# Rotary embedding and attention scores: the first batch in 24 KB stores, an early load on ScalarE's ring, and an uneven last store

## The chip, the cores and the metric

One core of a Trainium2 chip runs the kernel. The metric is the device time of one execution in microseconds (us). Runs of a kernel scatter by some 0.2 per cent here, so each comparison rests on five or six runs of a kernel with the kernel before run beside it. Instants are counted from the start of the profiled span, as in the views.

## The reference

For 16 batches of 512 positions, 16 heads of 64 numbers, q and k are rotated by tables of cosines and sines, and for each position and head the products with all 512 rotated k of that head are written out: 67 MB are read, 268 MB are written, all in float32.

```python
batch, seq, heads, dim = 16, 512, 16, 64
q_rot = concat([q1*cos - q2*sin, q1*sin + q2*cos])      # k_rot likewise
scores = einsum('bshd,bthd->bsht', q_rot, k_rot)         # (16, 512, 16, 512)
```

## The kernel before

The 512 positions of a batch lie as 128 partitions x 4 "slots". VectorE (DVE) rotates, TensorE (PE) transposes and multiplies, ScalarE (ACT) copies the products from PSUM to a staging buffer, and SyncE (SP) stores it: 4 MB for each of 64 slots, 32 KB per partition. There are three staging buffers of 4 MB. In the first batch one of them first holds the early inputs. A semaphore counts what has landed of each transfer: a "landing" is the moment at which one of the 16 DMA engines has finished its part, and "the median engine" is the middle of the 16. A "ring" is the queue of transfers that one issuing engine (SP or ScalarE) feeds.

```python
stage_pool = ctx.enter_context(tc.tile_pool(name="stage", bufs=3))
st_first = [stage_pool.tile([P, H, S], fp32, tag="stage", name="st") for _ in range(2)]
early = stage_pool.tile([P, 2 * C * H * D], fp32, tag="stage", name="early")
# ... cut
for head, heads in ((0, G), (G, H - G)):      # 4 heads of all rows, then 12
    load_units("k", head, heads)              # all on nc.sync
    load_units("q", head, heads)
load("k", 1); load("q", 1)
# ... cut; in scores(), first batch: unit i is 4 heads of all four slots, 1 MB per slot
if b == 0 and p % 2 == 1:
    c = p // 2
    nc.sync.dma_start(o_v[0, c, :, G * i : G * (i + 1)], st[:, G * c : G * (c + 1)])
elif b > 0 and p == HP - 1:
    nc.sync.dma_start(o_v[b, i % C], st)      # 4 MB
```

## Time and profile before

| | |
|---|---|
| Time, median of the runs beside the changed kernel | 802.22 us |
| Span of the profiled run | 799.2 us |
| Busy: PE, ACT, DVE | 86, 70, 68 per cent |
| DMA | 336.17 MB, mean 421 GB/s |

The views that bound it stand in the prediction. Two more are needed as a base for comparison. The first is DVE's timeline near 10 us (start, duration, engine, line, operation; in brackets the idle time before it and who ended it):

```profile
8.05 1.29 DVE L111 TENSOR_TENSOR early<-early,part 128x512 f32<-128x512 f32 x2
9.38 1.23 DVE L106 TENSOR_TENSOR part<-early,ss_t 128x1024 f32<-128x1024 f32 x1
```

The second is a table of short windows; its last two columns are the mean busy share of the 16 DMA engines and GB/s. Between 28 and 36 us, and about 60 us, the DMA engines are full:

```profile
28.00:30.00 2.00, 2.00 (x14) 0.91 (x12) 1.55 (x3) 1.42 (x3) 0.00 (x0) 1.00 1.01 430
30.00:32.00 2.00, 2.00 (x13) 1.14 (x12) 2.00 (x3) 1.36 (x2) 0.00 (x0) 1.00 1.08 426
32.00:34.00 2.00, 2.00 (x12) 0.99 (x12) 1.93 (x4) 1.91 (x4) 0.00 (x0) 1.00 0.88 377
34.00:36.00 2.00, 2.00 (x13) 0.77 (x10) 1.93 (x4) 2.00 (x4) 0.00 (x0) 1.00 1.04 430
...
60.00:62.00 2.00, 2.00 (x16) 1.31 (x16) 1.93 (x3) 2.00 (x4) 0.00 (x0) 1.00 1.03 422
```

### The profile page before, as it was taken

The numbers are of one execution on the slowest core, as the hardware profiler recorded it, in microseconds if no ns is written. First come the engines' busy times: TensorE is split into PE (matmuls) and PEld (weight loads), VectorE is DVE, ScalarE is ACT, GpSimd is POOL, SyncE is SP. The second block draws the span as 40 slices with busy tenths as digits, with TensorE's granted clock in tenths as the row PEclk, the third lists the DMA queues.
The fourth block names the chain that finished last, engine by engine and source line by source line (L and its number), as shares of the span: only waits on it lengthen the run. The fifth ranks groups of instructions, "written<-read, shape, count | busy, mean of one in ns | idle before, by whom it ended". The sixth has DMA issues, their size and how long they took to land.

```text
span 799.2 us, 7712 instructions
## 1 busy us (share of the span) xinstructions
PE 690.9 (86%) x3072; PEld 299.7 (37%) x3072; DVE 544.6 (68%) x516; ACT 561.8 (70%) x647; POOL 0.7 (0%) x6
## 2 busy tenths in 40 slices
PE   4989998997979789797897978979789897889970
PEld 2444443443434334343343433434334343334420
DVE  7999987676858568585684866848668586685300
ACT  3878886776848578585775856768567685667870
POOL 0000000000000000000000000000000000000000
PEclk9999999899989899898998989989899898998995
DMA  9999999999999999999999999999999999998995
GB/s 353 420 426 430 431 416 430 426 433 440 424 438 423 428 435 424 442 425 433 427 433 431 432 431 429 433 433 424 426 428 435 433 402 430 438 426 362 429 422 249
DMA packets 17700, 336.17 MB, mean 421 GB/s; under 512 B 1792, under 2 KB 3072, under 8 KB 4096
## 3 DMA queue, kind: packets, MB, share of 16 engines
q1 hardware_dynamic: 17376, 335.55, 98.4%
q8 instruction: 24, 0.39, 0.2%
q10 hardware_dynamic: 288, 0.13, 0.1%
q14 instruction: 12, 0.10, 0.0%
HBM read 67.24 MB, written 268.44 MB: 420 GB/s over the span
## 4 chain that ended last, share of the span: by engine, by line
DMA 50%; PE 37%; DVE 5%; ACT 4%; issue 1%; ACTq 0%; DVEq 0%
DMA out_dram<-st 49%; PE ps L155 28%; PE bank L127 9%; ACT st L162 4%; DVE part L106 2%; DVE early L111 1%; DVE k_sb L107 1%; DVE k_sb L111 1%; DVE early L107 1%; DMA early<-in_k_dram 1%; DVE kT_t L142 0%; DVE q_sb L107 0%; DVE q_sb L111 0%; ACTq L270 0%; DVE qT_t L142 0%
## 5 line engine op out<-in xcount | busy, mean ns | idle before, releaser
L162 ACT COPY st<-ps 128x1024 f32<-128x1024 f32 x512 | 495.3, 1018 | 202.8 <-DMA out_dram<-st 113.9
L155 PE MATMUL ps<-kT_t,qT_t 64*128 64x512 f32 x2048 | 548.6, 654 | 70.9 <-ACT st L162 70.9
L155 PEld LDWEIGHTS ps<-kT_t,qT_t 64*128 64x128 f32 x2048 | 185.4, 198 | 258.9 <-issue 138.9
L142 DVE COPY qT_t<-bank 128x512 f32<-128x512 f32 x118 | 81.6, 691 | 202.4 <-PE bank L127 202.4
L127 PEld LDWEIGHTS bank<-ident,q_sb 128*128 128x128 f32 x480 | 55.6, 152 | 104.5 <-issue 101.9
L127 PE MATMUL bank<-ident,q_sb 128*128 128x128 f32 x480 | 86.8, 309 | 0.9 <-PE ps L155 0.9
L127 PEld LDWEIGHTS bank<-ident,k_sb 128*128 128x128 f32 x480 | 50.5, 141 | 95.1 <-DVE k_sb L107 38.0
L127 PE MATMUL bank<-ident,k_sb 128*128 128x128 f32 x480 | 78.7, 287 | 1.6 <-DVE qT_t L142 1.2
L142 ACT COPY kT_t<-bank 128x512 f32<-128x512 f32 x122 | 72.4, 597 | 6.2 <-PE bank L127 6.2
L107 DVE TENSOR_TENSOR q_sb<-q_sb,cos_t 128x1024 f32<-128x1024 f32 x60 | 73.5, 1225 | 2.1
L111 DVE TENSOR_TENSOR k_sb<-k_sb,part 128x1024 f32<-128x1024 f32 x60 | 73.5, 1225 | 2.1
L107 DVE TENSOR_TENSOR k_sb<-k_sb,cos_t 128x1024 f32<-128x1024 f32 x60 | 73.5, 1225 | 2.0
L106 DVE TENSOR_TENSOR part<-q_sb,ss_t 128x1024 f32<-128x1024 f32 x60 | 73.5, 1225 | 2.0
L106 DVE TENSOR_TENSOR part<-k_sb,ss_t 128x1024 f32<-128x1024 f32 x60 | 73.0, 1216 | 0.1
L111 DVE TENSOR_TENSOR q_sb<-q_sb,part 128x1024 f32<-128x1024 f32 x60 | 72.9, 1216 | 0.0
L127 PE MATMUL bank<-ident,early 128*128 128x128 f32 x64 | 10.5, 316 | 12.2 <-DVE early L111 10.3
L127 PEld LDWEIGHTS bank<-ident,early 128*128 128x128 f32 x64 | 8.3, 161 | 17.6 <-issue 14.3
L106 DVE TENSOR_TENSOR part<-early,ss_t 128x1024 f32<-128x1024 f32 x8 | 9.8, 1223 | 5.7 <-ACT ss_t L187 5.5
L111 DVE TENSOR_TENSOR early<-early,part 128x512 f32<-128x512 f32 x16 | 10.3, 687 | 0.2
L107 DVE TENSOR_TENSOR early<-early,cos_t 128x1024 f32<-128x1024 f32 x8 | 9.8, 1224 | 0.3
L142 ACT COPY qT_t<-bank 128x512 f32<-128x512 f32 x10 | 5.6, 615 | 3.2 <-PE bank L127 3.2
L142 DVE COPY kT_t<-bank 128x512 f32<-128x512 f32 x6 | 4.1, 685 | 1.3 <-PE bank L127 1.3
(9 smaller groups left out, 2.8 us busy)
## 6 DMA issues: line engine op xcount, KB each, us to landing
out_dram<-st SPq DMA_DIRECT2D x60, 4096.0 KB, 25.0
k_sb<-in_k_dram SPq DMA_DIRECT2D x15, 2048.0 KB, 28.4
q_sb<-in_q_dram SPq DMA_DIRECT2D x15, 2048.0 KB, 27.5
out_dram<-st SPq DMA_DIRECT2D x16, 1024.0 KB, 13.0
early<-in_k_dram SPq DMA_DIRECT2D x1, 1536.0 KB, 9.1
early<-in_q_dram SPq DMA_DIRECT2D x1, 1536.0 KB, 12.3
early<-in_k_dram SPq DMA_DIRECT2D x1, 512.0 KB, 4.7
early<-in_q_dram SPq DMA_DIRECT2D x1, 512.0 KB, 5.4
```

Of the source, the lines that this page charges most:

```text
L106: nc.vector.tensor_tensor(pv, xs, ss, op=mult)
L107: nc.vector.tensor_tensor(xc, xc, cs, op=mult)
L111: nc.vector.tensor_tensor(y, y, z, op=add)
L127: nc.tensor.transpose(bank[:, x, :], src, ident)
L142: copy(out=dst, in_=src)
L155: nc.tensor.matmul(out=po, lhsT=lhs[64 * r : 64 * r + 64, :], rhs=rh, start=True, stop=True)
L162: nc.scalar.copy(out=so, in_=si)
```

## The change

It has three parts with three aims (`...` marks what is left out): larger store packets in the first batch (four heads of all slots first, then the other twelve heads slot by slot, 24 KB per partition); an earlier start (the first 0.5 MB of q is issued by ScalarE, on its own ring, beside SP's); and a shorter end (part of the last store is given to few DMA engines, so that a slow one has less to do).

```diff
-            load_units("k", head, heads)
-            load_units("q", head, heads)
+            load_units(nc.sync, "k", head, heads)
+            load_units(nc.scalar if head == 0 else nc.sync, "q", head, heads)
...
+        dve = rope("k", 1) + rope("k", 2) + rope("k", 3) + rope("r", 0)
+        for p in range(HP):                    # four heads of all slots
+            c, hp = divmod(p, 2)
+            scores(qT["q", 0][:, C * hp + c], kT[0][:, hp], st_first[0][:, 2 * p : 2 * p + 2], True)
+            if hp == 1:
+                nc.sync.dma_start(o_v[0, c, :, :G], st_first[0][:, G * c : G * (c + 1)])
+            if p in (3, 7):
+                load("kq"[p // 4], 2)
...
         for i in range(C):                     # twelve heads, slot i
-            st = st_first[i] if i < 2 else stage_pool.tile(...)
+            st = st_first[1] if i == 0 else stage_pool.tile(...)
...
+            for p in range(2, HP):
+                scores(qT["r", i][:, p], kT[0][:, p], st[:, 2 * p : 2 * p + 2], True)
...
+            nc.sync.dma_start(o_v[0, i, :, G:], st[:, G:])
...
+    def store(i, st):
+        o = o_v[i // C, i % C]
+        if i < NST - 1:
+            nc.sync.dma_start(o, st)
+            return
+        h = H - 2
+        nc.sync.dma_start(o[:, :h], st[:, :h])
+        nc.sync.dma_start(o[:116, h:], st[:116, h:])
+        nc.sync.dma_start(o[116:, h:], st[116:, h:])
```

## The prediction

> **What bounds the kernel now.** I read the page's slices first, then the DMA issues, the end of the span in windows of 2 us, the landing events of each transfer, and the timelines of SP, ACT and PE in the first 80 us.
>
> ```profile
> DMA  9999999999999999999999999999999999998995
> GB/s 353 420 426 430 431 416 430 426 433 440 424 438 423 428 435 424 442 425 433 427 433 431 432 431 429 433 433 424 426 428 435 433 402 430 438 426 362 429 422 249
> ...
> HBM read 67.24 MB, written 268.44 MB: 420 GB/s over the span
> ```
>
> The DMA engines are full from the second slice to the last but one, at some 430 GB/s, with no compute engine over 86% busy. So it is a DMA kernel, and only three things can move its time: bytes or packets, stretches in which an engine has nothing queued, and the ends. The change alters no bytes. The end is the odd part:
>
> ```profile
> 787.00:789.00 2.00, 0.00 (x0) 0.00 (x0) 0.00 (x0) 0.00 (x0) 0.00 (x0) 0.50 0.87 377
> 789.00:791.00 2.00, 0.00 (x0) 0.00 (x0) 0.00 (x0) 0.00 (x0) 0.00 (x0) 0.50 0.69 295
> 791.00:793.00 2.00, 0.00 (x0) 0.00 (x0) 0.00 (x0) 0.00 (x0) 0.00 (x0) 0.50 0.08 33
> 793.00:795.00 2.00, 0.00 (x0) 0.00 (x0) 0.00 (x0) 0.00 (x0) 0.00 (x0) 0.50 0.08 33
> ```
>
> The last two columns are DMA share and GB/s: for some 7 us a share near 1/16 is left, that is one engine, sending 32 KB packets one after another (1213 ns each in the trace). I call it the straggler. Each transfer raises its semaphore once for each engine, so the 16 landings show who lags. On the last store the last engine lands 7.4 us after the median one, the second 1.8 us, the third 1.3 us. Going back: the last engine's lag is 2.4 us at 88 us, 2.7 at 170, 4.0 at 270, 7.3 at 440, 10.3 at 728, then 7.3 because the others ran dry for 3 us there. From about 200 us on one engine alone falls behind by 0.2 to 0.3 us a store. As its lag is never zero, it never waits: **the time is this engine's work, plus whatever idle time it has early on.** The dip in slice 37 costs nothing for the same reason.
>
> The first batch, as SP issues it:
>
> ```profile
> 20.03 3.71 SPq L165 DMA_DIRECT2D out_dram<-st  x2
> 23.79 0.49 SPq L79 DMA_DIRECT2D k_sb<-in_k_dram  x1
> 25.22 9.39 SPq L165 DMA_DIRECT2D out_dram<-st  x4
> 34.67 1.06 SPq L79 DMA_DIRECT2D q_sb<-in_q_dram  x1
> 36.12 27.43 SPq L165 DMA_DIRECT2D out_dram<-st  x10
> 63.65 1.08 SPq L79 DMA_DIRECT2D k_sb<-in_k_dram  x1
> 74.62 20.37 SPq L167 DMA_DIRECT2D out_dram<-st  x3
> ```
>
> and the only wait of ScalarE for a buffer in it:
>
> ```profile
> 40.90 2.85 ACT L162 COPY st<-ps 128x1024 f32<-128x1024 f32 x3 [1.98 <-DMA out_dram<-st]
> ```
>
> Sixteen 1 MB stores keep the queue 4 to 11 us ahead: the first full store is issued at 74.6, and the load before it lands at 78.3. ScalarE waits 2 us at 40.9 for the slowest engine (median landing 38.8), which hurts nobody.
>
> **What the Trainium skill says.** (1) "DMA: Bandwidth & Descriptors", section "Why a DMA increments its semaphore by 16 and not by 1": a transfer uses the largest k up to 16 that divides the slowest dimension of both sides, on the lowest-numbered engines. So 116 rows run on engines 0 to 3 (29 rows each), 12 rows on engines 0 to 11. All transfers of before have 128 rows, and the trace has 16 landings for each; no run here shows k=4 yet. (2) The same page, "Latency and other measured facts": engines 7 and 15 are usually slower than the others. The trace agrees that one engine is; its number is not recorded. (3) The same page, "Issuing engines are not separate DMA queues": issuing from two engines saves only issue time; here an issue takes 0.60 to 0.66 us. (4) "TensorE: Matmul & The Clock Gate", "What's actually happening": one idle window of about 3.4 us halves the clock. The trace agrees: after idling 2.83 us PE restarts at 720.04 and the clock stands at 0.5 from 719.4 to 726.2.
>
> **The change part by part.**
>
> *Start.* q's first 0.5 MB leaves SP's ring, so SP's later loads go out some 0.65 us earlier (one issue). The engines' shares in the 1 us windows from 2 to 4 us are 0.72 and 0.86, so at most 0.14 + 0.28 = 0.4 us is there. I take -0.3 us. The DVE start (5.53 us) waits for the sine table, not for q.
>
> *Packets.* Twelve of sixteen first-batch stores become four of 3 MB. An 8 KB packet takes 309 ns, a 32 KB one 1213, so 24 KB about 911 (estimate by interpolation). Each engine swaps 96 packets of 309 (29.7 us) for 32 of 911 (29.2 us): -0.5 us.
>
> *Early work, new order.* DVE works straight through: k0 and q0 end at 13.2 as now; then k1, k2, k3 (3.8 us each) end at 24.7, the 768-wide rope (0.75 of 1.22 us, three times) at 27.6, k4 at 31.3, and so on; it is ahead. ScalarE: the first block's last eviction ends at 28.0, then the four copies of k3 and of q's slot 0 at 30.1, six evictions (0.95 us pitch) and four transposed copies, 7.8 us a slot: slot 0's store is issued at 38.7. Queued for DMA until then: loads to 24.1 - 0.3, four 1 MB stores at 2.45, two 2 MB loads at 4.8: to 43.3. Fine, so far.
>
> Now the buffers. There are three: one holds the 1 MB stores, one slot 0, the third the early inputs, until slot 3 takes it. Slot 1 reuses the first (slowest landing about 40.4): evictions 40.4 to 48.2. Slot 2 reuses slot 0's, and **must wait for the 3 MB store to land**: that runs 43.3 to 50.6 on the median engine and, with the 2 us lag that the trace has at that time, to 52.5. Then 7.8 us of ScalarE: 60.4, plus 1.4 us from issue to first packet (0.73 to about 2.1 at the start): 61.8. But slot 1's store ends at 57.9 on the median engine, 59.8 on the slowest. **So the engines idle 2 to 4 us.** Slot 3 follows at 68.4 + 1.4 = 69.8 against 69.2: 0.6 us more. Then k's 2 MB load goes first (77.1 to 82.0), slot 4 is ready at 78.5, and the queue stays ahead. The first full store lands at 82.0 + 9.7 = 91.7 in place of 88.3 on the median engine: +3.4 us, with the start's 0.3 and the packets' 0.5 in it. The straggler of later was probably no laggard then (at +0.25 us a store it went from nothing to the 2 us pack between 88 and 187 us), so I give it nearly all of it: +3 us, range +1 to +4.
>
> *End.* The last store becomes 28 KB rows on all engines (8 packets of some 1062 ns, by the same interpolation), 29 rows of 4 KB (about 159 ns, between 121 for 3 KB and 309 for 8 KB) on engines 0 to 3, and one such row on engines 0 to 11. Engines 12 to 15: 8 x 1062 = 8.50 us in place of 8 x 1213 = 9.70, so -1.2. Engines 4 to 11: -1.05. Engines 0 to 3: 8.50 + 30 x 0.159 = 13.3, so +3.6 us, inside the straggler's 7.4 us lag. If the straggler is 15 (or 7), the end moves by -1.2.
>
> Sum: +3.0 - 1.2 = +1.8 us over 802.4, about 804. An author who chose 116 and 12 has probably measured something, and my chain rests on 2 us of slack, so I shade it down: 803.5.
>
> **The rivals.** *No dry spell:* if ScalarE's slots are 1 us shorter, or the lag at 50 us is small (it was 0.7 for the third engine), slot 2's store comes in time and the time is 802.4 - 0.8 - 1.2 = 800.4. For it: all of this is 2 us in a chain of 60. Against: the three-buffer wait is certain from the code, and 3 MB landing pieces are coarse. *Cold PE:* slot 2's wait leaves PE idle some 4 us, and a clock at 0.5 for 3.4 or 6.8 us, as at 720, adds 1 to 1.5 us to the dry spell: 805 to 806. For it: an idle of 2.45 us before 685.4 was already followed by 0.5. Against: a slot with six pairs is bound by ScalarE. *The straggler is one of engines 0 to 3:* then the end costs +3.6 where I have -1.2: 808. Against: the page's 7/15, and the evident aim of the split. *Straggler already lagging at 58 us:* it loses only 2 us: 802.5.
>
> **Range and chances.** 800.4 and 806 bracket the likely cases, 808 is the poor one: 799.5 to 807.5. Two per cent is 16 us; nothing here is near that, unless slots on all engines fall out of step for the whole run. Faster 0.01, same 0.97, slower 0.02.
>
> **What would show it.** Right: ScalarE waits some 4 us for an output store near 48 us, SP issues the third 3 MB store near 60, a DMA share clearly under 1 near 58 to 62 us; the first full store lands near 92; at the end twelve engines stop, four go on some 4.6 us, and one another 2 to 3. Wrong: a share of 1 throughout 50 to 70 us (no dry spell), 4 engines in the tail that include the last (wrong straggler), or a lag on the last store that is not about 7 us, which would mean that the straggler is not a fixed engine.

## The result and the profile after

The changed kernel took 807.15 us (median of 6 runs, 806.05 to 808.88) beside 802.22 for the kernel before: ratio 1.0064, interval 1.0049 to 1.0078. It is slower by 5 us, inside the stated range of 799.5 to 807.5 but at its edge, and 3.65 us over the point. A ratio here is the mean time of one kernel's fast runs over that of the other's of the same rounds, so not quite the ratio of the quoted medians. The profiled run has a span of 804.3 us.

The page's slices say where to look. The second to fifth slices (20 to 100 us), which had 420, 426, 430 and 431 GB/s, moved 394, 405, 343 and 412; of the rest no slice is as far below:

```profile
DMA  9998999999999999999999999999999999998996
GB/s 356 394 405 343 412 427 433 436 420 437 425 427 433 424 437 428 436 422 433 435 423 437 430 434 428 429 436 424 430 427 435 431 408 429 427 436 359 419 438 275
```

**The dry spell is there.** ScalarE's timeline has the wait for slot 0's store, SP's has the third of the four 3 MB stores (issued after 62 us; the group of four runs from 40.84 to 70.6), and the windows show engines without work:

```profile
47.25 1.01 ACT L183 COPY st<-ps 128x1024 f32<-128x1024 f32 x1
54.28 2.84 ACT L183 COPY st<-ps 128x1024 f32<-128x1024 f32 x3 [6.02 <-DMA out_dram<-st]
```

```profile
40.84 29.72 SPq L239 DMA_DIRECT2D out_dram<-st  x4
70.67 0.37 SPq L83 DMA_DIRECT2D k_sb<-in_k_dram  x1
80.25 20.37 SPq L160 DMA_DIRECT2D out_dram<-st  x3
```

```profile
58.00:60.00 2.00, 2.00 (x9) 0.94 (x6) 1.93 (x3) 1.84 (x3) 0.00 (x0) 0.50 0.50 213
60.00:62.00 2.00, 2.00 (x11) 1.07 (x11) 1.97 (x2) 1.45 (x4) 0.00 (x0) 0.94 0.03 12
62.00:64.00 2.00, 2.00 (x10) 0.59 (x8) 1.93 (x3) 2.00 (x3) 0.00 (x0) 1.00 0.48 201
```

The missing shares add up to (0.50 + 0.97 + 0.52) x 2 = 4.0 us. PE had idled 4.39 us, and the third column from the end shows its clock at 0.50 from 58 to 60 us. After it all engines start slot 2's store together, so that the lag of the slow ones is lost there once.

**The q load came late.** The listing of DMA issues has, as last number, the time from issue to landing; it was 5.4 us for this load before:

```profile
early<-in_q_dram ACTq DMA_DIRECT2D x1, 512.0 KB, 10.6
```

```profile
8.07 1.29 DVE L118 TENSOR_TENSOR early<-early,part 128x512 f32<-128x512 f32 x2
12.37 1.23 DVE L113 TENSOR_TENSOR part<-early,ss_t 128x1024 f32<-128x1024 f32 x1 [3.01 <-DMA early<-in_q_dram]
```

I had looked at when the load is issued, not at what it shares the engines with. The Trainium skill has this in "DMA: Bandwidth & Descriptors", section "Queues, rings and completion order": each DMA engine takes turns between the rings that have work, packet by packet. The trace agrees: in the 2 us windows from 6 to 12 us the engines start 177, 204 and 128 packets of q (1 KB, ScalarE's ring) and 200, 190 and 203 of 3 KB on SP's ring (k's 1.5 MB until 9.2 us, then q's). On one ring, in the kernel before, q had landed at 6.3 us (median engine) and k's 1.5 MB at 10.5; on two, k's 1.5 MB landed at 9.7 and q at 12.0. Taking turns is not all of it: q's first packet started at 5.8 us in place of 4.5, behind the two tables on ScalarE's ring, whose last packet started at 4.5.

**Two loads are slow.** By the packets of the trace, the 2 MB load of k for batch 2 (from 28.6 us) and that for batch 3 (from 78.9 us) took 1.19 and 1.30 us longer per engine than 8 packets at 611 ns; before it was 0.19 and 0.28. I call this the excess of a load. Its 16 KB packets take 0.61 us at first; then, for some 2 to 3 us (32 to 34.5, and 82 to 85 us), most take 0.7 to 1.3 us, on all engines. I had not foreseen this. In the windows, full engines move 270 GB/s there:

```profile
32.00:34.00 2.00, 1.90 (x10) 0.96 (x12) 1.97 (x2) 1.04 (x3) 0.00 (x0) 1.00 1.03 270
82.00:84.00 2.00, 2.00 (x14) 0.84 (x10) 1.40 (x2) 1.48 (x3) 0.00 (x0) 1.00 1.10 270
```

**The end is as predicted.** Eleven engines stop between 796.1 and 798.2, the four of the 116-row piece (engines 0 to 3, see the closing list) end at 801.4 to 802.3, and the slow one at 803.3:

```profile
796.00:798.00 2.00, 0.00 (x0) 0.00 (x0) 0.00 (x0) 0.00 (x0) 0.00 (x0) 0.50 0.41 129
798.00:800.00 2.00, 0.00 (x0) 0.00 (x0) 0.00 (x0) 0.00 (x0) 0.00 (x0) 0.50 0.32 127
800.00:802.00 2.00, 0.00 (x0) 0.00 (x0) 0.00 (x0) 0.00 (x0) 0.00 (x0) 0.50 0.28 102
802.00:804.00 2.00, 0.00 (x0) 0.00 (x0) 0.00 (x0) 0.00 (x0) 0.00 (x0) 0.50 0.01 2
```

A share of 0.31 is five of sixteen engines: the four and the slow one. (Its last 28 KB packet runs past 802; packets are booked where they start.)

### The profile page after: what moved, and what is told of

Same layout as the page of the kernel before. It is cut to its first block, busy times and chain, and to the rows that moved or that the text cites. A ratio compares the mean times of both kernels' runs of the same rounds, so it can differ in the third digit from the quotient of the medians.

```text
span 804.3 us, 7696 instructions
## 1 busy us (share of the span) xinstructions
PE 692.0 (86%) x3072; PEld 300.9 (37%) x3072; DVE 542.2 (67%) x510; ACT 564.5 (70%) x655; POOL 0.7 (0%) x6
## 4 chain that ended last, share of the span: by engine, by line
DMA 51%; PE 39%; ACT 6%; issue 0%; DVE 0%; ACTq 0%; DVEq 0%
DMA out_dram<-st 50%; PE ps L172 30%; PE bank L139 9%; ACT st L183 5%; DMA early<-in_q_dram 1%; ACT kT_t L155 0%; DVE part L113 0%; DVE early L114 0%; ACTq L296 0%; ACTq L195 0%; DVE early L118 0%; ACT qT_t L155 0%; ACTq L183 0%; DVEq L113 0%
## 5 line engine op out<-in xcount | busy, mean ns | idle before, releaser
L155 ACT COPY kT_t<-bank 128x512 f32<-128x512 f32 x128 | 75.8, 600 | 5.3 <-PE bank L139 5.3
L113 DVE TENSOR_TENSOR part<-early,ss_t 128x1024 f32<-128x1024 f32 (+1 forms) x9 | 10.0, 1106 | 8.8 <-ACT ss_t L203 5.5
L155 ACT COPY qT_t<-bank 128x512 f32<-128x512 f32 (+1 forms) x12 | 5.8, 544 | 6.8 <-PE bank L139 6.8
L118 DVE TENSOR_TENSOR early<-early,part 128x512 f32<-128x512 f32 (+1 forms) x14 | 10.3, 765 | 0.3
L114 DVE TENSOR_TENSOR early<-early,cos_t 128x1024 f32<-128x1024 f32 (+1 forms) x9 | 10.0, 1106 | 0.3
```

Of the source, the lines that this page charges most:

```text
L113: nc.vector.tensor_tensor(pv, xs, ss, op=mult)
L114: nc.vector.tensor_tensor(xc, xc, cs, op=mult)
L118: nc.vector.tensor_tensor(y, y, z, op=add)
L155: copy(out=dst, in_=src)
```

## The experiments

Eleven runs were made, ten of new kernels and one of the changed kernel again, all correct, each five rounds. Theory A is the prediction's: a dry spell from a buffer wait, and a slowest engine that sets the end. The rivals are in the expectations.

**e1: the change with q's first load back on SP's ring.**

```diff
-            load_units(nc.scalar if head == 0 else nc.sync, "q", head, heads)
+            load_units(nc.sync, "q", head, heads)
```

> The changed kernel with the first q load back on SP's ring. In the changed kernel's trace that load landed 10.6 us after its issue, at 12.4 us, and DVE waited 3.0 us for it. Theory A (the dry spell comes from slot 2 waiting for slot 0's 3 MB store to land, and that landing is set by the DMA queue, which was full until 45 us): q is roped 3 us earlier and slot 0's store is issued near 38.7 instead of 40.8 us, but it starts no earlier, so the time stays within 0.7 us of the changed kernel, 806.5 to 807.5, and ScalarE still waits 5 to 7 us near 48 us. Theory B (the late q load is what cost the time): about 3 us less, 804. Theory C (the 24 KB pattern makes packets slow): as A.

Measured: 805.04 us (before 801.68), ratio 1.0042, interval 1.0030 to 1.0054. Against 1.0064 and 1.0076 for the whole change that is some 2 us less, so the ring costs more than theory A allowed, and the time lies between what A and B had said. ScalarE's wait for slot 0's store is still there (4.80 us), and so is the slow k load near 78 us (1.27 us), but that near 29 us has gone (0.37).

**e2: the change with its last store whole.**

```diff
-        h = H - 2
-        nc.sync.dma_start(o[:, :h], st[:, :h])
-        nc.sync.dma_start(o[:116, h:], st[:116, h:])
-        nc.sync.dma_start(o[116:, h:], st[116:, h:])
+        nc.sync.dma_start(o, st)
```

> The changed kernel with its last store whole. The split gave the slowest engine 28 KB + 4 KB instead of 8 x 32 KB rows at the end, an estimated 1.05 us. Theory A: 1.0 us more than the changed kernel, about 808.2, and one engine alone at the end for some 7 us. If the split is useless or harmful (rival): the same or 1 us less.

Measured: 807.55 us, ratio 1.0080, interval 1.0066 to 1.0093. It is above the whole change's 1.0064, but level with its second measurement (1.0076, e11 below). By times alone it leaves the split open between nothing and 1.3 us; the sign fits. In its trace one engine ends alone, 8.1 us after the median one.

**e3: the kernel before with the split last store alone** (the three lines above, in place of the whole store).

> The kernel before with the split last store alone. Theory A: 1.05 us less than before, about 801.2 (ratio 0.9987); in its trace twelve engines stop, engines 0 to 3 some 4.5 to 6 us later, the slowest one last. Rival (the slowest engine is one of 0 to 3): 3.6 us more.

Measured: 800.70 us, ratio 0.9992, interval 0.9980 to 1.0004. The median is 1.0 us lower, as expected, and the interval still holds 1. In the trace ten engines end by 788.5 and an eleventh at 792.0, the four of the 116-row piece at 791.7 to 792.4, the slow one at 797.0.

**e4: the kernel before with q's first load on ScalarE's ring alone** (the edit of e1, the other way round).

> The kernel before with the first q load on ScalarE's ring alone. Theory A: that load lands near 12 us instead of 7 and DVE waits 3 us, but the DMA queue is 4 to 11 us ahead, so the time moves by less than 0.7 us, 801.9 to 802.9. Theory B: about 3 us more, 805.

Measured: 803.96 us, ratio 1.0033, interval 1.0021 to 1.0045. The ring costs 2.3 us by itself. But theory B's way (DVE late, stores late) is not it: the first full store is still issued well ahead (76.5 us, and the load before it lands at 79.7), and no window is dry. What the windows show is the slow load of k:

```profile
28.00:30.00 2.00, 2.00 (x14) 0.84 (x10) 1.97 (x2) 2.00 (x4) 0.00 (x0) 1.00 1.05 360
30.00:32.00 2.00, 2.00 (x10) 0.94 (x12) 2.00 (x4) 1.42 (x2) 0.00 (x0) 1.00 1.07 426
32.00:34.00 2.00, 2.00 (x14) 1.16 (x12) 1.97 (x4) 1.36 (x3) 0.00 (x0) 1.00 1.06 270
34.00:36.00 2.00, 2.00 (x12) 0.88 (x10) 1.97 (x3) 1.91 (x4) 0.00 (x0) 1.00 0.84 332
```

The engines are as busy as before, but three of the four windows move 270 to 360 GB/s, where before all four had 377 to 430. This load landed 5.9 us after the store ahead of it (median engine), 4.5 before. The median engine stays 1.4 us late to the end (last store at 792.40 in place of 790.97). The slowest engine lost another 1.6 us in this run, which one trace does not explain. A possible source of such differences is in every trace: 24 packets of 16 KB on the queue that the page calls "instruction". In the traces of before and of the change each took 0.9 to 1.0 us of its engine and lengthened the packets beside it, 1.3 to 1.9 us in all. One of them, at 69.65 us, is why one engine landed slot 2's store at 73.3 in the changed kernel's trace, and the others by 71.4. Whether they explain the 1.6 us is not shown.

**e5: the kernel before with q's first load late, but on SP's ring** (order k, k, q, q instead of k, q, k, q).

```diff
-        for head, heads in ((0, G), (G, H - G)):
-            load_units("k", head, heads)
-            load_units("q", head, heads)
+        for which, head, heads in (("k", 0, G), ("k", G, H - G), ("q", 0, G), ("q", G, H - G)):
+            load_units(which, head, heads)
```

> The kernel before with the first q load issued by SP after k's remaining 1.5 MB, so that q lands near 11 to 12 us as it does from ScalarE's ring, but on SP's ring. The ring alone had cost 2.3 us (803.96 against 801.68), and in all three traces with the ring the k load that starts near 29 us was slow (its packets 1.1 to 1.3 us longer in all per engine; 0.1 to 0.4 in the three without). Theory D (lateness: everything shifts by some 2 us and k's load falls into other traffic): 803 to 804.5 and the slow k load again. Theory E (the second ring itself leaves something behind): 801.2 to 802.4 and a k load with under 0.5 us of excess.

Measured: 802.61 us (before 801.21), ratio 1.0017, interval 1.0005 to 1.0030, and the slow k load again, 1.24 us of excess. The time lies between the two ranges; the slow load is what D had said and E had excluded. q landed at 10.8 us, and DVE waited 1.5 us for it. So a late q on SP's own ring also comes with the slow load and a cost of 1.4 us; no second ring is needed for it. That e4 is dearer than e5 is not established (the intervals overlap).

**e6: the first-batch reorder alone** (the change with the edits of e1 and e2 together).

> The first-batch reorder alone (q on SP's ring, last store whole). Theory A: the dry spell near 58 to 62 us of some 4 us on the median engine, and the slow k load near 78 to 84 us that all three traces with slots have (1.3 us): 4 to 5 us over before, 805.7 to 806.7; the three parts then add up to the whole change. Rival (the parts interact): under 3 us or over 6.

Measured: 805.21 us, ratio 1.0051, interval 1.0038 to 1.0063: 4.0 us. The trace has ScalarE's wait (5.34 us), the dry spell, and the slow k load near 78 us (1.24 us), and none near 29 us (0.12):

```profile
56.00:58.00 2.00, 2.00 (x8) 0.49 (x5) 1.97 (x2) 2.00 (x5) 0.00 (x0) 0.50 0.87 373
58.00:60.00 2.00, 2.00 (x12) 1.33 (x13) 1.93 (x3) 1.82 (x5) 0.00 (x0) 0.91 0.13 53
60.00:62.00 2.00, 2.00 (x12) 0.77 (x8) 1.97 (x2) 2.00 (x3) 0.00 (x0) 1.00 0.43 184
```

The parts add up: 0.51 (slots) + 0.33 (ring) - 0.08 (end) = 0.76 per cent, beside 0.64 and 0.76 measured for the whole.

**e7: e6 with batch 2's q load behind slot 0's store.** Slot 0's store then no longer stands behind this load, so that it should land by the time slot 2 needs its buffer.

```diff
-            if p in (3, 7):
-                load("kq"[p // 4], 2)
+            if p == 3:
+                load("k", 2)
...
             nc.sync.dma_start(o_v[0, i, :, G:], st[:, G:])
+            if i == 0:
+                load("q", 2)
```

> e6 with batch 2's q load moved behind slot 0's store in SP's order, so that this store starts near 40 instead of 44 us and lands near 49 instead of 53. Theory A (slot 2's wait for that landing makes the dry spell): slot 2's store is issued near 57, the queue has work until 59.5, no dry spell near 60, and the time falls by 2.5 to 4 us against e6, to 802 to 804. Rival (the 24 KB pattern itself is slow, not the wait): within 1 us of e6. If the slow k load near 80 us is tied to the dry spell before it, it vanishes with it, and the time is at the lower end.

Measured: 802.68 us, ratio 1.0018, interval 1.0004 to 1.0031: 2.5 us less than e6, at the weak end of what was expected. The wait for slot 0's store and the dry spell are gone:

```profile
58.00:60.00 2.00, 2.00 (x11) 0.77 (x9) 1.93 (x3) 2.00 (x4) 0.00 (x0) 1.00 0.94 401
60.00:62.00 2.00, 2.00 (x14) 1.26 (x14) 1.93 (x3) 2.00 (x4) 0.00 (x0) 1.00 0.99 418
```

The k load near 75 us is no longer slow (0.02 us), but now the moved q load, from 46.7 us, is (1.60 us), about as much as is left over before (1.5 us). Packets of 24 KB as such cost nothing: 912 ns each, near the 911 that the prediction interpolated.

**e8: the kernel before with four heads of the last store on the lowest-numbered engines.**

```diff
+                h = H - 4
+                nc.sync.dma_start(o[:, :h], st[:, :h])
+                for r0, r1 in ((0, 119), (119, 126), (126, 128)):
+                    nc.sync.dma_start(o[r0:r1, h:], st[r0:r1, h:])
```

> The kernel before with four heads of the last store on the lowest-numbered engines only: 119 rows (7 engines), 7 rows (7 engines), 2 rows (2 engines). In the changed kernel's trace the last landing of the 12-row piece (12 engines) came 0.19 us after the slowest engine's main piece, and none of the 116-row piece (engines 0 to 3) did, so the slowest engine is one of 4 to 11. If it is 7 or higher (7 is one of the two that the skill names as slow): it loses 8 x 8 KB at the end, 2.4 us, while engines 0 to 6 gain 3.2: 799.3, ratio 0.997. If it is 4, 5 or 6: it gains 3.2 us, 805.

Measured: 805.19 us, ratio 1.0049, interval 1.0037 to 1.0062: 4.0 us more, so the slow engine is among the seven. The trace shows it directly: of the 119-row piece six engines land between 792.5 and 794.0 and the seventh at 801.5. The tail is one engine again:

```profile
794.00:796.00 2.00, 0.00 (x0) 0.00 (x0) 0.00 (x0) 0.00 (x0) 0.00 (x0) 0.50 0.05 16
796.00:798.00 2.00, 0.00 (x0) 0.00 (x0) 0.00 (x0) 0.00 (x0) 0.00 (x0) 0.50 0.06 25
798.00:800.00 2.00, 0.00 (x0) 0.00 (x0) 0.00 (x0) 0.00 (x0) 0.00 (x0) 0.50 0.07 29
```

Together with the changed kernel, whose 116-row piece on engines 0 to 3 had landed 0.8 us before the slow engine's own, it is engine 4, 5 or 6, if pieces go to the lowest-numbered engines, as the Trainium skill has it ("DMA: Bandwidth & Descriptors", section "Why a DMA increments its semaphore by 16 and not by 1"; the traces do not number the engines), and if the slow engine is the same one on the two chips used (e8 ran on another chip than e3).

**e9: three heads of the last store on engines 0 to 3 only.**

```diff
+                h = H - 3
+                nc.sync.dma_start(o[:, :h], st[:, :h])
+                nc.sync.dma_start(o[:124, h:], st[:124, h:])
+                nc.sync.dma_start(o[124:, h:], st[124:, h:])
```

> The kernel before with three heads of the last store on engines 0 to 3 only (124 rows and 4 rows, both divide by 4). Taken together, the tails of the changed kernel (slowest engine not in 0 to 3) and of the 119-row kernel (in 0 to 6) put the slowest engine at 4, 5 or 6. Then it loses 8 x 6 KB = 1.8 us at the end, engines 0 to 3 gain about 32 x 0.235 - 1.8 = 5.7 us and still end before it if its lag is over 7.5: 799.5 to 800.3, ratio 0.998. Rival (another engine, or the small-k rule is not as the skill has it): 4 us or more over before.

Measured: 801.93 us (before 801.18), ratio 0.9998, interval 0.9985 to 1.0012: no gain, and not the 4 us of the rival either. In the trace the slow engine ended at 796.5, but the four of the small pieces at 795.7 to 797.4: they now set the end, one of them having come 1 us after the next. The piece was too large. The two-head piece leaves them 0.8 us or more of room (the changed kernel 0.8, e3 4.4 us).

**e10: the change with batch 2's k load issued behind the fourth 1 MB store.** In the traces up to here, a load was slow where SP issued a store 0.8 to 1.5 us after the load's first packet, so this moves the load away from such an issue.

```diff
-            if p in (3, 7):
-                load("kq"[p // 4], 2)
+            if p == 7:
+                load("k", 2)
+                load("q", 2)
```

> The changed kernel with batch 2's k load issued behind the fourth 1 MB store, beside q's. In all kernels with a late q this load was slow when SP issued a store 0.8 us after it had begun; in those without, the nearest store was issued 0.2 to 1.3 us before it began. Theory F (a store issued just inside a load's transfer makes the load slow): now no store is issued while k's load runs (34 to 39 us), its excess falls under 0.4 us, and the time falls by about 1 us against the changed kernel, unless q's load behind it takes the place (slot 0's store is issued near 41). Theory G (the first load after the first stores is slow when all is late): its excess stays over 1 us, the time within 0.7 us of the changed kernel.

Measured: 808.15 us, ratio 1.0082, interval 1.0070 to 1.0094: no gain. k's load is fast now (0.17), and q's behind it, with a store issued 1.24 us into it, is slow (1.06): the slowness moved, as the expectation had allowed. This fits theory F, but other loads contradict it: q's load in the changed kernel (store 1.29 us into it, excess 0.05), and k's load near 73 us in e9 (0.79 us into it, only 0.59). What makes a load slow stays open.

**e11: the changed kernel again.**

> The changed kernel unchanged, on the same chip and rounds as e10, and a second profile of it. All theories: 806 to 807.5, the dry spell near 60 us, and slow k loads near 29 and 79 us (over 1 us each); if the slow loads were chance, they lie elsewhere.

Measured: 807.80 us (before 801.18), ratio 1.0076, interval 1.0062 to 1.0090, 0.3 us above what was expected. Its second profile has the same dry spell (213, 12 and 201 GB/s in the three windows from 58 us) and slow k loads at 28.6 (1.07 us) and 79.0 us (1.17 us): they came at the same places twice, which speaks for the kernel's order and against chance.

The traces add up to the times. In them the slowest landing of the first full store, 90.8 us before, is later by 1.5 (e4), 1.9 (e5), 4.5 (e6), 1.0 (e7), 6.7 (e2) and 6.4 us (the change); the medians of the times rose by 2.3, 1.4, 4.0, 1.5, 5.9 and 4.9 us, the last with about 0.9 us gained back at the end. One trace each, they agree within 0.8 us; so most of the cost arises in the first 100 us.

No version beats both kernels clearly. The best is e3, the kernel before with the split last store: 800.7 us, 0.08 per cent below it, with an interval that includes no gain.

## Why the prediction was right or wrong

The range held, the direction was right, and the whole was too optimistic by 3.65 us: a change of +1.1 us was expected and +4.9 measured. That the range held was partly luck. Its upper part was meant for a straggler among engines 0 to 3, which was not so; two costs that the prediction did not have filled it instead, the late q with its slow load and the slow load near 79 us. The second measurement of the changed kernel (807.80) lies just outside. By its steps:

- **What bounds the kernel: right.** DMA, and within it one slow engine. In all kernels one engine lands last, 7 to 10 us after the median one; in the thirteen traces, 458 to 512 packets of some 7,600 of 32 KB took over 1230 ns (median 1249 to 1252, against 1213), about one engine's share of 480. That they are one engine's is inferred, since packets carry no engine number; 38 ns for each of 8 packets make 0.3 us, the step by which the lag grows at most stores.
- **Start, "-0.3 us": wrong, and the largest miss.** The step looked at the 0.65 us of issue time and did not ask what the load shares the engines with. Measured: q lands at 12.3 us instead of 6.8, DVE waits 3.0 us, and the part costs 2.3 us (e4). DVE's delay leaves no gap in the queue, as e4's windows show; what is seen is k's load at 29 us, slow in the kernels with a late q (e4, e5, e2, the change and e11) and in none with q in time. In e10, where this load was moved, it was fast and the next one slow. The slow load explains some 1.1 to 1.4 of the 2.3 us, the rest is open, and the link from late to slow is only correlated.
- **Packets, "-0.5 us": right in size by the packets** (912 ns against three of 309), but never seen alone.
- **Dry spell, "2 to 4 us": right.** On the median engine slot 1's last packet ended at 59.5 us (57.9 foreseen) and slot 2's first began at 63.5 (61.8 foreseen): 4.0 us dry, with 3.9 foreseen. For the slowest it was 2.5, with 2.0 foreseen. Everything was some 2 us later than written, 1.2 us of it through the slow k load. e7 shows the cause: with slot 0's landing earlier, wait and spell vanish and 2.5 us come back. The rival with a straggler that lags already at 58 us was right about this step, and is hidden in the time by the two slow loads.
- **First full store, "+3.4 us": +7.1** on the median engine (95.5 against 88.4), and +6.4 on the slowest, where +3 was written. The two k loads are most of the difference: from the store ahead of each to its own landing they took 6.0 and 6.2 us on the median engine, 4.5 and 4.9 before, 2.8 us more in all; another 0.4 is in slot 3's store, whose 24 KB packets took 1.00 us on average instead of 0.91.
- **Cold PE:** it happened (clock 0.50 from 54 to 60 us), and cost little: slot 2 took 8.3 us of ScalarE instead of 7.8. (The idle times of 2.45 and 2.83 us that the prediction cites are shorter than the window of 3.4 us that it sets beside them, and the clock was halved all the same; "the trace agrees" holds for the halving, not for the length.)
- **End, "-1.2 us" or -1.05: right in mechanism, and 0.8 to 1.0 us by the traces; the times support it weakly** (e3 -1.0 us, interval -1.6 to +0.3). From its landing before to its last one the slow engine took 9.7 us with a whole last store (before, e2 and e4 to e7), and 8.7 to 8.9 with the split one, the 4 KB row included (the change, e1, e3, e10 and e11). The four engines of the 116-row piece ended 5.2 to 6.0 us after the median one, where 4.8 was written. The guess that the slow engine is 15 or 7 was wrong, under the conditions at e8; it is outside 0 to 3, and so it gains.
- **"I shade it down": wrong.** Crediting the author's odd numbers with a measurement moved the point half a microsecond the wrong way.
- **Small slips.** Slot 3 is ready at 60.4 + 7.8 = 68.2, not 68.4. And "0.2 to 0.3 us a store" leaves out the stores at which the others lost time too: from 206 to 728 us the lag grew by 7.4 us over 43 stores, 0.17 each.

Of the rivals, the one without a dry spell fell, cold PE added little, and the straggler in 0 to 3 was refuted by the tail.

## What to carry to other kernels

In a kernel that only the DMA queue bounds, ask of each larger store what waits for its landing: with three buffers, a 3 MB piece lands late enough to stop the engine that fills the next one, although fewer, larger packets were the aim. A small urgent load belongs ahead of the bulk on the same ring (q landed at 6.8 us there); on a second ring it takes turns with whatever bulk is on the first (12.3 us). And look for the one slow DMA engine by comparing the sixteen landings of a transfer, before trusting mean busy shares.

## What the Trainium skill lacked or had wrong

- "DMA: Bandwidth & Descriptors", section "Issuing engines are not separate DMA queues", says that transfers issued from several engines interleave, and that this only saves sequencer time. What it lacks is what interleaving costs a small urgent load: here 0.5 MB took 10.6 us to land from the second ring, 5.4 from the first, and the kernel before lost 2.3 us by it (e4). The page's account of taking turns between rings, cited above, explains most of the landing.
- The same page, section "Latency and other measured facts", names engines 7 and 15 as usually slower, with a guess that involves software-generated descriptors. Here, where SP and ScalarE issue every transfer of the program, one engine is slower, 1251 against 1213 ns for 32 KB as inferred above, and the landings put it among 4 to 6 under the conditions given at e8.
- No page has the slow loads: 16 KB load packets of mostly 0.7 to 1.3 us instead of 0.61, on all engines, for some 2 to 3 us (1.1 to 1.6 us lost per load), at the same places in both traces of the changed kernel, and moving to another load when the order changes.
- Not lacking, but a check: what the page says of pieces with few rows (section "Why a DMA increments its semaphore by 16 and not by 1") held: the 116-row piece made four landings plus one early update for the other twelve, the 12-row piece twelve plus one, the 119-row piece seven plus one.
